# Where the sums of the feed-forward weights are formed: VectorE's additions in four buffers, or adding DMAs in two

## The chip, the cores and the metric

The kernel runs on one core of a Trainium2 chip. The metric is device time in microseconds (us) of the whole program; the median of three executions before the change is 2494.41 us (2494.4 to 2494.79). The engines are named as the profile names them: PE is TensorE (matmuls), PEld its weight loads, DVE VectorE, ACT ScalarE, POOL GpSimd, and SP SyncE, whose queue issues nearly all DMAs here. A line such as L1243 is a line of the kernel.

## The reference

One step of a hybrid decoder layer of width 1024, for 2048 prompt tokens and 8 sample sequences of 8 tokens, which share the weights:

```python
h = rmsnorm(x, norm_mix_w)
proj = h @ w_in          # rq, rk, rv, rg (RetNet), hq, hf, hi, hg (HGRN2), 512 columns each
o_r, s_ret = chunk_gla(rotary(rq), rotary(rk) * 128**-0.5, rv, log(1 - 2**(-5-h)), s_ret0)
f = lb + (1 - lb) * sigmoid(hf)
o_h, s_hg = chunk_gla(silu(hq) * 128**-0.5, 1 - f, hi, log(f), s_hg0)
o = concat(head_rmsnorm(o_r) * silu(rg), head_rmsnorm(o_h) * silu(hg))
x = x + o @ w_out
h = rmsnorm(x, norm_ffn_w)
x = x + square(relu(h @ w_up)) @ w_down      # 1024 -> 4096 -> 1024
y = rmsnorm(x, final_norm_w)
```

`chunk_gla` is a gated linear recurrence in chunks, four heads of each kind with 128 dimensions. Everything is float32, and the four new states are outputs too.

## The kernel before

**Arithmetic.** The kernel forms each float32 product from split operands: every weight and activation is cut into a high part (`hi`, a float32r copy by ACT, L270 for weights) and the rest (`lo`, a subtraction by DVE, L284), and three matmuls (hi by hi, hi by lo, lo by hi) add up in PSUM.

**Order.** Tokens go in three groups of 640, 768 and 704 columns (the last holds the 64 sample rows). First all three groups are mixed: projection (L341), values (L748), the two recurrences and the output projection. Then come three groups of feed-forward (L1211). Group 0 is mixed up to about 394 us, group 1 to about 820 us, group 2 to about 1188 us; the feed-forward takes the rest.

**Feed-forward.** Up and down matrices are cut into 16 sets (8 of each) of four weight tiles A11, A12, A21, A22, each 128x1024 float32 (512 KB). Instead of eight block products, seven are made, by a scheme of Strassen's kind. It needs sums of weight tiles and sums of activation blocks:

```python
S1 = A21 + A22;  S2 = S1 - A11;  S3 = A11 - A21;  S4 = A12 - S2
T1 = B12 - B11;  T3 = B22 - B12; T2 = T3 + B11;   T4 = B21 - T2
PRODUCTS = A11*B11, S2*T2, A12*B21, S3*T3, S1*T1, A22*T4, S4*B22
```

The S sums are made once, in `plan_sums`, while groups 1 and 2 are being mixed (eight sets in each), stored in DRAM tiles `su...` and `sd...` and loaded in the feed-forward as other weights are. The T sums are made by `block_sum` for each group of the feed-forward.

**What sets the order of instructions.** The program is emitted in one pass, and a counter of ticks runs along: one tick for every two matmuls of a projection (three of the values). `plan_sums` puts steps with due ticks in a list, `self.side`; `tick` emits a step when its tick has come, among whatever the mixing emits there. Each engine then runs its own instructions in that order (the steps of the sums are held in program order), so an instruction that waits holds back all that follow it on its engine or queue. Sets start at tick 16 and at 141 + 192*(j//2) + 85*(j%2): after the first, two sets for each 192 ticks, which is one head pair of the mixing. Within a set the steps stand so: loads of A21 and A22 at 0, A11 at 12, A12 at 24 (L1240, SP); S1 at 40, S3 at 50, S2 at 60, S4 at 70 (L1243, DVE); stores at 60, 70, 80, 90 (L1248, SP). The tiles come from a pool with the tag "sum" and four buffers, one set's worth. SP's queue carries, in between, the loads of the weights for the mixing, some of them already split halves kept in DRAM (`w16hi`, `w16lo` and so on, L253).

Other lines that the text speaks of: ACT's evictions L357, its tables L361 and L363, its copies L505, its gate L854; PE's column sums L511 and L512, which need a PSUM bank that L357 empties; POOL's tensor products L705, L713, L894 and L895.

Of the kernel before, what the change touches and what calls it, by code (L numbers as in the profile page):

```python
# [9 lines left out]
F32 = mybir.dt.float32  # L10
F32R = mybir.dt.float32r
U8 = mybir.dt.uint8
AF = mybir.ActivationFunctionType
ALU = mybir.AluOpType

P = 128
# [26 lines left out]
WT = 1024  # L43
# [15 lines left out]

T_SUMS = {"T1": ("B12", ALU.subtract, "B11"), "T3": ("B22", ALU.subtract, "B12"), "T2": ("T3", ALU.add, "B11"),
          "T4": ("B21", ALU.subtract, "T2")}
QUARTER = {(0, 0): "B11", (0, 1): "B12", (1, 0): "B21", (1, 1): "B22"}
PLACE = {name: q for q, name in QUARTER.items()}
A_PLACE = {"A11": 0, "A12": 1, "A21": 2, "A22": 3}
# [133 lines left out]
class Kernel:  # L200
# [36 lines left out]
    def load(self):  # L237
        return self.ld.tile([P, SLAB], F32, tag="ld", name="ld")
# [993 lines left out]
    def plan_sums(self, sets, starts):  # L1232
        nc, w = self.nc, self.I["w"]
        assert not self.side
        self.side = deque()

        def load(x, i, *names):
            for name in names:
                x[name] = self.wp.tile([P, WT], F32, tag="sum", name="raw", bufs=4)
                self.tc.keep_in_program_order(nc.sync.dma_start(x[name], w[i + A_PLACE[name]]))  # L1240

        def make(x, name, a, op, b, into):
            self.tc.keep_in_program_order(nc.vector.tensor_tensor(out=x[into], in0=x[a], in1=x[b], op=op))  # L1243
            x[name] = x[into]

        def keep(x, key, name):
            s = self.sums[key + (name,)] = self.dp.tile([P, WT], F32, name="s" + "".join(map(str, key)) + name)
            self.tc.keep_in_program_order(nc.sync.dma_start(s, x[name]))  # L1248

        for start, (key, i) in zip(starts, sets):  # L1250
            x, t = {}, self.n_ticks + start
            steps = [(0, load, x, i, "A21", "A22"), (12, load, x, i, "A11"), (24, load, x, i, "A12"),
                     (40, make, x, "S1", "A21", ALU.add, "A22", "A22"),
                     (50, make, x, "S3", "A11", ALU.subtract, "A21", "A21"),
                     (60, make, x, "S2", "S1", ALU.subtract, "A11", "A11"),
                     (70, make, x, "S4", "A12", ALU.subtract, "S2", "A12")]
            steps += [(d, keep, x, key, name) for d, name in ((60, "S1"), (70, "S3"), (80, "S2"), (90, "S4"))]
            for d, fn, *a in sorted(steps, key=lambda z: z[0]):
                self.side.append((t + d, lambda fn=fn, a=a: fn(*a)))
        self.side = deque(sorted(self.side, key=lambda z: z[0]))  # L1260

    def out_proj(self, g, when, beside, between=lambda: None):
# [45 lines left out]
        return first, second  # L1308

    def block_sum(self, g, B, name):  # L1310
        a, op, b = T_SUMS[name]
        s = self.get()
        self.nc.vector.tensor_tensor(out=s[:, :g.T], in0=B[a][:, :g.T], in1=B[b][:, :g.T], op=op)  # L1313
        B[name] = s

    def plan_operands(self, g):

# [510 lines left out]
```

## Time and profile before

| | |
|---|---|
| median of three executions | 2494.41 us |
| profiled execution, first to last instruction (span) | 2490.7 us |
| difference of the two | 3.7 us |
| mean granted TensorE clock | 0.999 |
| PE, PEld busy | 2478.4, 2461.9 us (100%, 99%) |
| DVE, ACT, POOL busy | 1868.8, 1246.4, 377.3 us (75%, 50%, 15%) |
| 16 DMA engines, mean busy share of the sync queue's transfers | 62.3% |
| DMA bytes | 525.44 MB |

A group row of the profile reads: line, engine, operation, output tile and input tiles, shapes, count, then busy time and mean ns of one, then the idle time of the engine just before these instructions and what ended it. A row of the waits reads: engine, line, what it waited for; us in total, how often, the longest. A row of a timeline reads: start, duration, engine, line, operation, tiles, how many like it were merged, and in brackets the idle time before it with what ended it; for SP the duration is that of issuing, not of the transfer. A row of DMA issues gives count, KB of each, and the median us from issue to landing.

### The profile page before, as it was taken

Reading aid. Unit: us, or ns where it says so; the run is one execution under the profiler, and the core shown is the slowest. Engines: PE = TensorE matmul, PEld = TensorE weight load, DVE = VectorE, ACT = ScalarE, POOL = GpSimd, SP = SyncE. Lnnn points to the kernel's source line nnn. Section 1 sums busy time; section 2 is a strip of 40 time slices with the busy share of each in tenths; the row PEclk is TensorE's granted clock in tenths of the full one; section 3 lists DMA queues with packets and bytes.
Section 4 is the critical chain, followed back from the end, with each engine's and each line's share of the span. In section 5 each row is a group of like instructions: output and inputs, shape, how many; then the busy total and the mean of one; then the engine's idle time right before and its main releaser. Section 6 shows DMA issues by size and latency. Waiting matters only on the chain.

```text
span 2490.7 us, 41430 instructions
## 1 busy us (share of the span) xinstructions
PE 2478.4 (100%) x16520; PEld 2461.9 (99%) x16520; DVE 1868.8 (75%) x2453; ACT 1246.4 (50%) x1674; POOL 377.3 (15%) x320
## 2 busy tenths in 40 slices
PE   9999999999999999999999999999999999999998
PEld 9999999999999999999999999999999999999998
DVE  7666766667685666686775899776699878778987
ACT  6665663444464444453644545444454436445544
POOL 5223304324421442340000000000000000000000
PEclk9999999999999999999999999999999999999999
DMA  7454575465566665768876866576675545867552
GB/s 265 166 185 170 203 259 178 161 229 186 184 210 236 220 219 200 266 211 270 283 213 221 280 198 213 174 239 222 203 262 177 188 151 190 288 196 247 194 189 89
DMA packets 191655, 525.44 MB, mean 211 GB/s; under 512 B 20963, under 2 KB 62563, under 8 KB 191462
## 3 DMA queue, kind: packets, MB, share of 16 engines
q1 hardware_dynamic: 191318, 522.77, 62.3%
q8 instruction: 130, 2.13, 0.4%
q14 instruction: 63, 0.52, 0.1%
q10 hardware_dynamic: 144, 0.02, 0.0%
HBM read 389.28 MB, written 132.39 MB: 209 GB/s over the span
## 4 chain that ended last, share of the span: by engine, by line
PE 98%; DVE 1%; DMA 0%; ACT 0%; issue 0%; SPq 0%; DVEq 0%
PE pj L341 29%; PE pf L1211 26%; PE pj L1211 25%; PE pjv L748 8%; PE mm L920 2%; PE mm L1108 1%; PE po L1100 1%; PE po L1102 1%; PE mm L977 1%; PE mm L512 1%; PE mm L511 1%; PE po L784 1%; PE mm L1034 1%; PE mm L850 1%; DMA lo<-w33lo 0%; DMA slab<-x 0%
## 5 line engine op out<-in xcount | busy, mean ns | idle before, releaser
L270 ACT CAST hi<-raw 128x1024 fp32r<-128x1024 f32 x392 | 411.8, 1050 | 616.6 <-PE pf L1211 258.4
L341 PE MATMUL pj<-slab,hi 128*128 128x320 f32 (+2 forms) x3072 | 661.4, 328 | 1.8 <-DVE slab L649 1.0
L1211 PE MATMUL pf<-slab,hi 128*128 128x320 f32 (+2 forms) x2768 | 657.6, 321 | 0.0
L1211 PE MATMUL pj<-slab,hi 128*128 128x352 f32 (+2 forms) x2608 | 620.6, 322 | 0.0
L284 DVE TENSOR_TENSOR lo<-raw,hi 128x1024 fp32r<-128x1024 f32 x392 | 485.6, 1239 | 113.6 <-ACT hi L270 108.1
L341 PEld LDWEIGHTS pj<-slab,hi 128*128 128x128 f32 x3072 | 508.3, 188 | 3.9 <-DVE slab L649 1.2
L1211 PEld LDWEIGHTS pf<-slab,hi 128*128 128x128 f32 x2768 | 480.1, 188 | 0.0
L1211 PEld LDWEIGHTS pj<-slab,hi 128*128 128x128 f32 x2608 | 452.9, 188 | 0.1
L1211 PE MATMUL pf<-slab,lo 128*128 128x320 f32 (+2 forms) x1384 | 444.1, 321 | 0.0
L1211 PE MATMUL pj<-slab,lo 128*128 128x352 f32 (+2 forms) x1304 | 419.1, 321 | 0.0
L341 PE MATMUL pj<-slab,lo 128*128 128x320 f32 (+2 forms) x1536 | 379.5, 327 | 0.5 <-DVE lo L284 0.4
L341 PEld LDWEIGHTS pj<-slab,lo 128*128 128x128 f32 x1536 | 263.6, 188 | 1.6 <-DVE lo L284 1.0
L1211 PEld LDWEIGHTS pf<-slab,lo 128*128 128x128 f32 x1384 | 259.6, 188 | 0.0
L1211 PEld LDWEIGHTS pj<-slab,lo 128*128 128x128 f32 x1304 | 244.6, 188 | 0.0
L748 PE MATMUL pjv<-hi,slab 128*128 128x256 f32 x1024 | 193.3, 285 | 0.0
L1302 ACT CAST slab<-slab 128x640 fp32r<-128x640 f32 (+2 forms) x192 | 145.2, 778 | 64.0 <-DVE slab L1313 51.7
L1306 DVE TENSOR_TENSOR slab<-slab 128x640 fp32r<-128x640 f32 (+2 forms) x192 | 167.0, 884 | 8.5 <-PE pj L1211 2.8
L748 PEld LDWEIGHTS pjv<-hi,slab 128*128 128x128 f32 x1024 | 162.2, 192 | 1.4
L748 PE MATMUL pjv<-lo,slab 128*128 128x256 f32 x512 | 144.8, 283 | 0.0
L899 ACT ACTIVATE slab<-slab 128x640 f32<-128x640 f32 (+2 forms) x72 | 56.3, 782 | 147.7 <-POOL slab L895 147.4
L1556 DVE TENSOR_TENSOR slab<-pf,slab 128x640 f32<-128x640 f32 (+2 forms) x88 | 77.5, 886 | 29.4 <-PE pf L1211 28.9
L748 PEld LDWEIGHTS pjv<-lo,slab 128*128 128x128 f32 x512 | 98.1, 192 | 0.0
(222 smaller groups left out, 3009.0 us busy)
## 6 DMA issues: line engine op xcount, KB each, us to landing
raw<-w SPq DMA_DIRECT2D x264, 512.0 KB, 4.3
slab<-u SPq DMA_DIRECT2D x32, 384.0 KB, 4.8
u<-ld SPq DMA_DIRECT2D x30, 384.0 KB, 4.0
slab<-u SPq DMA_DIRECT2D x32, 352.0 KB, 5.0
u<-ld SPq DMA_DIRECT2D x30, 352.0 KB, 3.9
slab<-u SPq DMA_DIRECT2D x32, 320.0 KB, 4.6
u<-ld SPq DMA_DIRECT2D x30, 320.0 KB, 4.3
ld<-x SPq DMA_DIRECT2D x16, 384.0 KB, 3.8
```

Source lines behind the costliest of these rows:

```text
L270: self.nc.scalar.copy(hi, raw)
L284: self.nc.vector.tensor_tensor(out=lo, in0=self.second.pop(j), in1=hi.bitcast(F32), op=ALU.subtract)
L341: self.nc.tensor.matmul(pj[:, i, :T2], w, a[:, c0:c1], start=j == 0 and q == 0, stop=j == n - 1 and q == 2)
L511: self.nc.tensor.matmul(ps, self.ones_r, hi, start=True, stop=False)
L512: self.nc.tensor.matmul(ps, self.ones_r, lo, start=False, stop=True)
L748: nc.tensor.matmul(pj[:, i * 256:(i + 1) * 256], a[:, s:s + C], ww, start=kb == 0 and q == 0, stop=kb == KB - 1 and q == 2)
L899: nc.scalar.activation(x["dd", w][:, a:T], x["dd", w][:, a:T], AF.Exp)
L920: nc.tensor.matmul(ps[:, j], qk[:, cols[c]], second(qk[:, cols[c]]), start=True, stop=True)
L1211: self.nc.tensor.matmul(*a, **k)
L1302: self.nc.scalar.copy(hi[:, :g.T], B[name][:, :g.T])
L1306: self.nc.vector.tensor_tensor(out=lo[:, :g.T], in0=B[name][:, :g.T], in1=hi.bitcast(F32)[:, :g.T], op=ALU.subtract)
L1556: nc.vector.tensor_tensor(out=r, in0=ps, in1=r, op=ALU.add)
```

## The change

The sums S are formed by DMAs that add to what stands in their destination (`accum_op`), issued from GpSimd's queue, and only A21 and A22 have buffers. In this way, with the signs that can be had by additions alone:

- SP loads A21 and A22 (ticks 0 and 1). ACT negates both in place, a Copy activation with scale -1 over 128x1024 (ticks 14 and 16).
- Tick 22: A22's buffer += A21's buffer, SBUF to SBUF, which makes -S1; stored at 34.
- Tick 36: A21's buffer += A11 from DRAM, which makes S3; stored at 48.
- Tick 46: A22's buffer += A11 from DRAM, which makes -S2; it may begin once the store of -S1 has landed; stored at 58.
- Tick 70: A22's buffer += A12 from DRAM, which makes S4; it may begin once the store of -S2 has landed; stored at 82.

S1 and S2 are negated, so T1 and T2 are, too: T1 is B11 - B12, T2 is -T3 - B11 in one scalar_tensor_tensor, T4 is B21 + T2. The seven products have the values they had. The pool with the tag "sum" keeps its four buffers, so that two sets fit in it. The starts of the sets are as they were. The scratch for dynamic DMAs is 512 instead of 256.

```diff
-T_SUMS = {"T1": ("B12", ALU.subtract, "B11"), "T3": ("B22", ALU.subtract, "B12"), "T2": ("T3", ALU.add, "B11"),
-          "T4": ("B21", ALU.subtract, "T2")}
+T_SUMS = {"T1": ("B11", ALU.subtract, "B12"), "T3": ("B22", ALU.subtract, "B12"), "T4": ("B21", ALU.add, "T2")}
...
-        def load(x, i, *names):
-            for name in names:
-                x[name] = self.wp.tile([P, WT], F32, tag="sum", name="raw", bufs=4)
-                self.tc.keep_in_program_order(nc.sync.dma_start(x[name], w[i + A_PLACE[name]]))
-        def make(x, name, a, op, b, into):
-            self.tc.keep_in_program_order(nc.vector.tensor_tensor(out=x[into], in0=x[a], in1=x[b], op=op))
-            x[name] = x[into]
...
+        def load(x, i, name):
+            x[name] = self.wp.tile([P, WT], F32, tag="sum", name="raw", bufs=4)
+            order(nc.sync.dma_start(x[name], w[i + A_PLACE[name]]))
+        def negate(x, name):
+            order(nc.scalar.activation(x[name], x[name], AF.Copy, scale=-1.0))
+        def add(x, name, term):
+            order(nc.gpsimd.dma_start(x[name], x[term] if isinstance(term, str) else w[term], accum_op=ALU.add))
...
-            steps = [(0, load, x, i, "A21", "A22"), (12, load, x, i, "A11"), (24, load, x, i, "A12"),
-                     (40, make, x, "S1", "A21", ALU.add, "A22", "A22"),
-                     (50, make, x, "S3", "A11", ALU.subtract, "A21", "A21"),
-                     (60, make, x, "S2", "S1", ALU.subtract, "A11", "A11"),
-                     (70, make, x, "S4", "A12", ALU.subtract, "S2", "A12")]
-            steps += [(d, keep, x, key, name) for d, name in ((60, "S1"), (70, "S3"), (80, "S2"), (90, "S4"))]
...
+            for d, fn, *a in ((0, load, i, "A21"), (1, load, i, "A22"), (14, negate, "A21"), (16, negate, "A22"),
+                              (22, add, "A22", "A21"), (34, keep, "A22", key + ("S1",)), (36, add, "A21", i + A_PLACE["A11"]),
+                              (46, add, "A22", i + A_PLACE["A11"]), (48, keep, "A21", key + ("S3",)),
+                              (58, keep, "A22", key + ("S2",)), (70, add, "A22", i + A_PLACE["A12"]),
+                              (82, keep, "A22", key + ("S4",))):
...
+        if name == "T2":
+            self.nc.vector.scalar_tensor_tensor(out=s[:, :T], in0=B["T3"][:, :T], scalar=-1.0, in1=B["B11"][:, :T],
+                                                op0=ALU.mult, op1=ALU.subtract)
+            return
...
-    nc = _bacc.Bacc("TRN2", target_bir_lowering=False, num_devices=1, dynamic_dma_scratch_size=256)
+    nc = _bacc.Bacc("TRN2", target_bir_lowering=False, num_devices=1, dynamic_dma_scratch_size=512)
```

More of the change, by code (lines that the diff above doesn't have):

```diff
@@ L1235, in plan_sums @@
         self.side = deque()
-        def load(x, i, *names):
-            for name in names:
-                x[name] = self.wp.tile([P, WT], F32, tag="sum", name="raw", bufs=4)
-                self.tc.keep_in_program_order(nc.sync.dma_start(x[name], w[i + A_PLACE[name]]))
-        def make(x, name, a, op, b, into):
-            self.tc.keep_in_program_order(nc.vector.tensor_tensor(out=x[into], in0=x[a], in1=x[b], op=op))
-            x[name] = x[into]
-        def keep(x, key, name):
-            s = self.sums[key + (name,)] = self.dp.tile([P, WT], F32, name="s" + "".join(map(str, key)) + name)
-            self.tc.keep_in_program_order(nc.sync.dma_start(s, x[name]))
+        order = self.tc.keep_in_program_order
@@ new lines, in load, with keep @@
+        def load(x, i, name):
[5 more added lines that the diff above has]
+            order(nc.gpsimd.dma_start(x[name], x[term] if isinstance(term, str) else w[term], accum_op=ALU.add))
+        def keep(x, name, key):
+            s = self.sums[key] = self.dp.tile([P, WT], F32, name="s" + "".join(str(k) for k in key))
+            order(nc.sync.dma_start(s, x[name]))
@@ L1257, in plan_sums @@
-            steps += [(d, keep, x, key, name) for d, name in ((60, "S1"), (70, "S3"), (80, "S2"), (90, "S4"))]
-            for d, fn, *a in sorted(steps, key=lambda z: z[0]):
-                self.side.append((t + d, lambda fn=fn, a=a: fn(*a)))
+            for d, fn, *a in ((0, load, i, "A21"), (1, load, i, "A22"), (14, negate, "A21"), (16, negate, "A22"),
[3 more added lines that the diff above has]
+                              (82, keep, "A22", key + ("S4",))):
+                self.side.append((t + d, lambda fn=fn, a=a, x=x: fn(x, *a)))
@@ L1310, in block_sum @@
     def block_sum(self, g, B, name):
+        s = self.get()
+        B[name], T = s, g.T
+        if name == "T2":
+            self.nc.vector.scalar_tensor_tensor(out=s[:, :T], in0=B["T3"][:, :T], scalar=-1.0, in1=B["B11"][:, :T],
+                                                op0=ALU.mult, op1=ALU.subtract)
+            return
         a, op, b = T_SUMS[name]
-        s = self.get()
         self.nc.vector.tensor_tensor(out=s[:, :g.T], in0=B[a][:, :g.T], in1=B[b][:, :g.T], op=op)
-        B[name] = s
     def plan_operands(self, g):
```

## The prediction

> **What bounds the kernel now.** I read in this order: busy time and the chain that ended last, then TensorE's (PE's) own waits, the busy time in the two stretches that hold the sums, and the timelines of SP, ACT and POOL where one set hands over to the next.
>
> ```profile
> span 2490.7 us, 41430 instructions
> PE 2478.4 (100%) x16520; PEld 2461.9 (99%) x16520; DVE 1868.8 (75%) x2453; ACT 1246.4 (50%) x1674; POOL 377.3 (15%) x320
> ...
> q1 hardware_dynamic: 191318, 522.77, 62.3%
> ...
> PE 98%; DVE 1%; DMA 0%; ACT 0%; issue 0%; SPq 0%; DVEq 0%
> ```
>
> PE is busy all the time and is 98% of the chain. What it waited for is the whole of this list:
>
> ```profile
> PE mm L408 <- DVE eps L412: 1.1, 1, 1.1
> PE pj L341 <- DVE slab L649: 1.0, 1, 1.0
> PE pf L1755 <- ACT slab L1746: 0.8, 1, 0.8
> PE pj L341 <- DVE slab L1271: 0.8, 1, 0.8
> PE pj L341 <- DVE lo L284: 0.4, 1, 0.4
> ```
>
> That is 4.1 us, none of it behind a weight sum (L1243) or its loads and stores. The sums are made in the mixing of groups 1 and 2; there the engines stood so (columns: busy us of PE, weight loads, DVE, ACT, POOL; clock; DMA share; GB/s):
>
> ```profile
> 394.00:820.00 426.00, 426.00 (x2933) 421.44 (x2932) 290.10 (x421) 198.55 (x290) 142.50 (x109) 1.00 0.56 199
> 820.00:1188.00 368.00, 367.01 (x2644) 361.76 (x2643) 255.61 (x442) 169.36 (x280) 115.95 (x109) 1.00 0.69 234
> ```
>
> PE has under 1 us free in 794 us, so time can only be lost here: there is nothing behind PE to give back. The measured median is 2494.4 us, which leaves 3.7 us outside the profiled span; I add changes to 2494.4.
>
> **The change part by part.**
>
> ```profile
> L1243 DVE TENSOR_TENSOR raw<-raw 128x1024 f32<-128x1024 f32 x64 | 90.2, 1410 | 0.3
> L270 ACT CAST hi<-raw 128x1024 fp32r<-128x1024 f32 x392 | 411.8, 1050 | 616.6 <-PE pf L1211 258.4 <-PE pj L1211 207.0 <-issue 76.3
> L1313 DVE TENSOR_TENSOR slab<-slab 128x768 f32<-128x768 f32 x32 | 29.7, 950 | 0.0
> L1401 DVE SCALAR_TENSOR_TENSOR ld<-ld 128x768 f32<-128x768 f32 x14 | 13.3, 950 | 0.0
> raw<-w SPq DMA_DIRECT2D x264, 512.0 KB, 4.3
> ```
>
> *DVE.* 64 additions go, 64 x 1.41 = 90.2 us of an engine that is 68% busy (290.1 of 426) where they stand and releases no PE wait there. Gain: 0. T2 as a SCALAR_TENSOR_TENSOR costs 950 ns as the TENSOR_TENSOR did; T1's turned sign costs nothing. Cover: DVE's free third.
>
> *ACT.* 32 negations of 128x1024 at 1.05 us (the same tile in L270) = 33.6 us on an engine half idle. Free by themselves. But each now waits in ACT's order for a load, and PE stands behind ACT; that price comes below.
>
> *The larger DMA scratch* adds no instruction: 0. *PE's own order:* in group 2 the sample heads' matmuls move a few places; 0, at most a wait of the size listed (1 us).
>
> *DMA traffic.* A set had four loads and four stores; it has two loads, four stores and four accumulates, of which three fetch from DRAM. 525 MB took 62.3% of 16 engines over 2490.7 us, so 0.524 MB takes 1.55 us of all of them; two to six more such passes per 44 us (an accumulate counted as one pass or two) make 3 to 9 us, which lifts the share of 0.56 to 0.69 by 0.07 to 0.2. It stays under 1 and prolongs other loads, at no cost of its own while these are fetched early.
>
> *The hand-over, where the change can cost.* In two buffers the sums form a chain, each step waiting for the one before: S1 is added in A22 (one accumulate) and kept, only then can A11 be added onto it (S2), kept, then A12 (S4), kept. Three accumulates (A) and two stores (S) are serial: x = 3A + 2S + five hand-overs. Behind it in SP's order stand the next set's two loads, and behind them in ACT's order that set's negations. In the profile:
>
> ```profile
> 502.31 5.60 SPq L1240 DMA_DIRECT2D raw<-w  x2
> 508.00 0.38 SPq L253 DMA_DIRECT2D hi<-w16hi  x1
> ...
> 590.41 5.05 SPq L1240 DMA_DIRECT2D raw<-w  x2
> ```
> ```profile
> 511.75 0.58 ACT L854 ACTIVATE slab<-mm,con 128x384 f32<-128x384 f32 x1 [0.84 <-PE mm L850]
> ```
> ```profile
> 545.56 0.52 ACT L505 CAST slab<-slab 128x384 fp32r<-128x384 f32 x1
> 546.10 1.28 ACT L361 ACT_TABLE_LOAD   x1
> 549.40 0.84 ACT L361 ACTIVATE slab<-slab 128x768 f32<-128x768 f32 x1 [2.02 <-DVE slab L649]
> 550.26 1.28 ACT L363 ACT_TABLE_LOAD   x1
> 552.18 0.58 ACT L357 ACTIVATE slab<-mm,eps 128x384 f32<-128x384 f32 x1 [0.64 <-PE mm L512]
> 555.63 0.58 ACT L357 ACTIVATE slab<-mm,eps 128x384 f32<-128x384 f32 x1 [2.31 <-PE mm L512]
> ```
>
> The loads of one pair of sets to the next are 590.41 - 502.31 = 88.1 us apart: 44 us a set, eight pairs in all (four per group; group 2 a little shorter). In each pair the first set's negations go in beside L854, done by about 513 (511.75 + 0.58 + the negation), and the first accumulate starts there. The second set's first negation stands right behind L505 (545.56 + 0.52 = 546.1). Its 1.05 us fit in ACT's 2.02 us wait before L361; beyond that the delay runs through L361 and the L357 of 552.18 to PE, whose next L511 (about 555.1, as the L357 it releases starts at 555.63) is in need of that bank some 2.3 us after L357 gave it up. So the second set's A21 must have landed by about 549.4. It is issued at 513 + x and takes a load's 4.3 us: nothing is lost up to x = 549.4 - 513 - 4.3 = 32.1. Above that ACT stands, PE behind it, and every us of x beyond 32.1 is a us of the kernel in each of eight pairs. From a second set to the next first set there are 88.1 - (549.4 - 513) = 51.7 us, which binds only when x is some 15 us longer.
>
> Now A and S. A store of a sum, alone and bunched, with the fastest and slowest landing of this line's transfers in one pair:
>
> ```profile
> su7S<-raw SPq DMA_DIRECT2D x4, 512.0 KB, 5.2
> sd00S<-raw SPq DMA_DIRECT2D x4, 512.0 KB, 7.2
> sd01S<-raw SPq DMA_DIRECT2D x4, 512.0 KB, 4.2
> sd20S<-raw SPq DMA_DIRECT2D x4, 512.0 KB, 5.7
> ...
> DMA to landing us min/median/max: 2.6/7.8/9.7
> ```
>
> S: 5.45, the middle of 4.2 to 7.2 and of the two between. Hand-overs: the issue of a DMA takes SP 0.32 to 0.38 us; five of them 1.6. No queue of GpSimd and no accumulate is in the trace (the queue that moves all but 3 MB is q1). The nearest row is the same 512 KB as a plain load, 4.3 us; a plain pass alone took 2.6, which is the lower end of A; two passes at the bunched worst, 19.4, are the upper. An accumulate reads two tiles and writes one where a copy reads and writes one: 1.5 x 4.3 = 6.5, or, if it goes as two passes, 8.6. I take the middle, 7.5, as an estimate.
>
> x = 3 x 7.5 + 2 x 5.45 + 1.6 = 35.0, which is 2.9 us over 32.1; times eight is 23 us: 2494.4 + 23 = 2517. The price turns on A: A = 6.5 gives x = 32.0 and no loss at all, A = 10 gives x = 42.5 and 83 us.
>
> The Trainium skill, Collectives: The Full Stack (Stop ④, why ReduceScatter is half of AllGather), says that an adding transfer is slower because it needs two source reads, and its DMA page, DMA: Bandwidth & Descriptors (Anatomy of one DMA), gives about 2.0 us plus bytes over 436 GB/s for a transfer from GpSimd. From these two, an estimate: 2.0 + 2 x 1.2 = 4.4 us for one accumulate that is alone, and by that A the sum would be 2494; no run here shows an accumulate.
>
> Other work behind the waits: SP's loads of hi/lo weights (w18 to w21) stand among the keeps, and POOL's tensor products (L705, L713, L894) behind the accumulates' waits. POOL is idle for two thirds of these windows (142.5 of 426), and the first of its products after the chain is wanted later than the second set's load, so they bind after it; taken as 0.
>
> **Rivals.**
>
> *Hidden: no change.* If A is 6.5 or less with S as taken, the chain ends in time, and ACT's waits and SP's fall in idle time. For it: the fastest landing is 2.6, and two loads a set bunch less than four. Against: the median in a pair was 7.8. Time 2494.4, within 2 us.
>
> *Accumulates far slower, chain over a set's whole share.* If GpSimd cannot feed its queue while VectorE works beside it, A grows towards 12 or more. Then the chain from loads to loads, 4.3 + 2.1 (two negations) + x, is the pace itself: at A = 12, x = 48.5 and the set 54.9 us, 10.9 over its 44; sixteen sets, 174 us: 2669. Decides from x = 44 - 6.4 = 37.6 on, A about 8.4. For it: DVE is 68% busy there. Against: no DMA of the trace, bunched with others, took over 9.7. The Trainium skill's SBUF — State Buffer (the "DVE blocks DMA" trap) states such a rule for DMAs issued from GpSimd: their descriptors cannot be written while VectorE runs an operation in a two-port mode. No trace here shows it yet.
>
> *Faster.* With 90 us off DVE, a PE wait on DVE in these two groups would go. The listed waits on DVE are 1.1 + 1.0 + 0.8 + 0.4 = 3.3 us; even all of them gone gives 2491.1, and by the windows only 1 us of it lies in the sums' stretches. It needs over 5 us to count as faster; only a change in how fast PE streams could do that, and I see none.
>
> **How the numbers follow.** A change below 0.2% (5 us) cannot be told from none; in eight pairs that is 0.6 us each, so x up to 32.7, A up to 6.7. Chances by A: up to 6.7, 0.38; 6.7 to about 10, the hand-over as the loss, 0.40; above 10, the chain as the pace, 0.18; faster 0.04. The forecast is the second: 2517, its own range 2500 to 2577 (A = 10). The range for 8 in 10 takes in the hidden case and ends just above the second: 2492 to 2580. Same 0.38, slower 0.58, faster 0.04.
>
> **What would show it.** L1243 gone from DVE, its busy time down by 90 us; 32 more Copy activations near 1.05 us. A queue of GpSimd with 64 issues, landing at about 7.5 us. In the waits, ACT waiting for a load at the second set of each pair, some 3 us each time, and PE's L511/L512 waiting on ACT's L357 eight times; SP standing before the keeps. Right on the mechanism and wrong on size if A is another; wrong altogether if PE waits for something else, such as a weight half (hi/lo) that SP fetched late behind a keep, or a POOL product behind an accumulate, or if PE slows with no wait at all.

## The result, and the profile after

The changed kernel takes 2559.97 us in the median of four runs (2555.32 to 2575.8), against 2494.49 us before (four runs): 1.0276 times the time, 95% interval 1.0261 to 1.0291, which is 65 us slower. The prediction said 2517 us, 2492 to 2580, slower with 0.58: side and range hold, the size is short by almost a factor of three. The profiled execution is the slowest of the four, 2575.8 us, 16 us above the median; what follows splits up this execution.

From its page, the span, TensorE's (PE's) line, the queue of GpSimd's DMAs and their landing times (median, us):

```profile
span 2574.0 us, 41479 instructions
PE 2513.3 (98%) x16520; PEld 2490.4 (97%) x16520; DVE 1810.2 (70%) x2389; ACT 1277.9 (50%) x1706; POOL 400.3 (16%) x384
...
q0 software_dynamic: 9216, 33.56, 7.6%
...
raw<-w POOLq DMA_DIRECT2D x48, 512.0 KB, 7.8
```

The span is 83.3 us longer than before. Of this 48.4 us are PE standing still (span less busy time, 60.7 us against 12.3), and 34.9 us are the same 16520 matmuls taking longer. In the two stretches of mixing that hold the sums (columns as before the change):

```profile
394.00:820.00 426.00, 402.90 (x2683) 396.30 (x2683) 248.34 (x375) 199.81 (x291) 138.43 (x130) 0.96 0.68 198
820.00:1188.00 368.00, 347.01 (x2417) 338.36 (x2416) 198.93 (x353) 166.82 (x263) 134.39 (x141) 0.96 0.79 226
```

PE is now idle 44 us in these 794 us, where it was idle for one, and the granted clock is 0.96 where it was 1.00. PE's own waits (what it waited for: us in total, times, longest) were five rows of 4.1 us; the largest now are:

```profile
PE mm L976 <- DVE slab L905: 16.8, 5, 4.0
PE po L783 <- POOL slab L776: 8.7, 3, 3.5
PE mm L510 <- ACT slab L356: 5.6, 3, 2.5
PE po L783 <- DMA ld<-hg_s: 5.3, 1, 5.3
PE pjv L741 <- DMA lo<-w5lo: 3.8, 1, 3.8
PE mm L510 <- ACT slab L504: 3.2, 3, 2.6
```

(The lines of this kernel are one lower than before up to the sums: L976 is the former L977, L356 the former L357.) Three things stand in this list, and a fourth behind it.

**VectorE held up by GpSimd.** The largest row ends in L905, a short product that VectorE forms of two tiles in SBUF. The minimum, median and maximum of L904, the product ahead of it, in ns, in the changed kernel and in the kernel before (there L905):

```profile
L904 DVE TENSOR_TENSOR slab<-slab x72: 477/547/8858, 48.7 to 1182.3; 128x320 f32<-128x320 f32 x40, 128x384 f32<-128x384 f32 x24, 128x352 f32<-128x352 f32 x8
```
```profile
L905 DVE TENSOR_TENSOR slab<-slab x72: 477/650/1258, 48.6 to 1107.8; 128x320 f32<-128x320 f32 x40, 128x384 f32<-128x384 f32 x24, 128x352 f32<-128x352 f32 x8
```

An operation of half a microsecond took 8.86. The timelines of VectorE and of GpSimd at that place:

```profile
504.09 8.86 DVE L904 TENSOR_TENSOR slab<-slab 128x384 f32<-128x384 f32 x1 [2.40 <-ACT slab L898]
512.88 0.55 DVE L905 TENSOR_TENSOR slab<-slab 128x384 f32<-128x384 f32 x1
```
```profile
502.35 0.84 POOL L894 TENSOR_TENSOR slab<-slab 128x384 f32<-128x384 f32 x1
503.83 0.89 POOL L1246 DMA_DIRECT2D raw<-w  x1 [0.64 <-DMA su2S<-raw]
504.43 1.51 POOL L948 TENSOR_TENSOR slab<-slab 128x384 f32<-128x384 f32 x1
...
511.36 1.17 POOL L894 TENSOR_TENSOR slab<-slab 128x384 f32<-128x384 f32 x1
```

GpSimd issues an adding DMA at 503.83 and then runs eight operations without a break until 512.53. (L893 and L894 are differences of two tiles, L948 and L926 products; "products" means the whole run here, as in the expectations.) VectorE's operation starts 0.3 us after that issue has begun and comes to its end 0.4 us after the run. This happens eight times, four in each group, with 6.2 to 10.1 us each (L904 three times, L951 three times, L713 twice; all of them combine two tiles in SBUF). In the kernel before, GpSimd has runs of 11 to 13 us at the same places, and 8 to 11 operations of VectorE fall into each, none longer than 2.2 us.

**The chain of a set, and what waits behind it.** From GpSimd's, SP's and ScalarE's timelines, the set su3:

```profile
531.59 0.89 POOL L1246 DMA_DIRECT2D raw<-raw  x1 [2.26 <-ACT raw L1243]
536.63 0.89 POOL L1246 DMA_DIRECT2D raw<-w  x1 [4.15 <-DMA raw<-raw]
...
545.48 0.89 POOL L1246 DMA_DIRECT2D raw<-w  x1 [6.46 <-issue]
...
558.22 0.89 POOL L1246 DMA_DIRECT2D raw<-w  x1 [9.98 <-DMA su3S<-raw]
```
```profile
564.89 0.32 SPq L1250 DMA_DIRECT2D su3S<-raw  x1
565.27 1.19 SPq L1240 DMA_DIRECT2D raw<-w  x2
```
```profile
571.00 1.06 ACT L1243 ACTIVATE raw<-raw 128x1024 f32<-128x1024 f32 x1 [5.60 <-DMA raw<-w]
```

From the first accumulate to the next set's loads 565.27 - 531.59 = 33.7 us; when the first of those loads has landed ScalarE's negation starts, at 571.0, ScalarE has stood still for 5.6 us, and PE then waits 2.5 us for L356. That is the step on which the prediction rested. But GpSimd stands in the same chain (10 us before 558.22), with L776 behind it in group 2; and SP stands in it, with weight halves (w5) and the sample states (hg_s) behind it.

**The clock.** PE's granted clock (last column but two) around three pauses of PE, of 4.04, 2.54 and 1.44 us:

```profile
509.44:513.50 4.06, 0.02 (x1) 0.03 (x1) 4.06 (x3) 0.06 (x1) 3.09 (x3) 0.80 0.00 0
513.50:516.00 2.50, 2.50 (x14) 2.38 (x15) 2.50 (x6) 2.08 (x4) 0.00 (x0) 0.50 0.00 0
516.00:518.00 2.00, 2.00 (x12) 1.66 (x12) 0.24 (x1) 0.43 (x2) 0.00 (x0) 0.50 0.00 0
518.00:520.00 2.00, 2.00 (x16) 2.00 (x16) 0.00 (x0) 0.00 (x0) 0.00 (x0) 0.81 0.17 29
```
```profile
574.57:577.11 2.54, 0.00 (x0) 0.00 (x0) 0.00 (x0) 2.50 (x4) 1.71 (x2) 0.93 0.00 0
577.11:579.11 2.00, 2.00 (x6) 2.00 (x7) 0.56 (x1) 1.42 (x3) 0.79 (x1) 0.50 0.39 80
579.11:581.11 2.00, 2.00 (x12) 2.00 (x12) 0.56 (x1) 0.29 (x2) 0.00 (x0) 0.73 0.95 186
479.85:482.00 2.15, 2.15 (x13) 2.15 (x14) 0.87 (x2) 1.61 (x3) 0.80 (x1) 1.00 0.46 93
```

After the pause of 4 us PE runs at half clock for nearly 5 us, which costs another 2.6 us; after 2.5 us it loses some 1.5 us; after 1.4 us nothing. Read in the same way in windows of half a microsecond, the profile has twelve such stretches in these two groups, each behind a pause of 2.5 us or more, and together they cost some 31 of the 34.9 us of longer matmuls (an estimate from PE's busy time and its clock in each window). Over the whole run that makes (48.4 + 34.9) / 48.4, about 1.7 times the length of the pauses.

### The profile page after: what moved, and what is told of

It is laid out like the page before. It is cut to its first block, busy times and chain, and to the rows that moved or that the text cites. A ratio compares the mean times of both kernels' runs of the same rounds, so it can differ in the third digit from the quotient of the medians.

```text
span 2574.0 us, 41479 instructions
## 1 busy us (share of the span) xinstructions
PE 2513.3 (98%) x16520; PEld 2490.4 (97%) x16520; DVE 1810.2 (70%) x2389; ACT 1277.9 (50%) x1706; POOL 400.3 (16%) x384
## 4 chain that ended last, share of the span: by engine, by line
PE 52%; DVE 0%; DMA 0%; ACT 0%; DVEq 0%; issue 0%
PE pf L1210 26%; PE pj L1210 24%; PE pj L340 2%; DMA ld<-hg_s 0%; DVE slab L1667 0%; PE po L783 0%; DVE slab L1766 0%; PE po L1101 0%; PE mm L1107 0%; PE po L1099 0%; PE pf L1759 0%; DVE slab L1624 0%; PE pj L511 0%; PE pj L510 0%; PE mm L834 0%; ACT slab L1700 0%
## 5 line engine op out<-in xcount | busy, mean ns | idle before, releaser
L340 PE MATMUL pj<-slab,hi 128*128 128x320 f32 (+2 forms) x3072 | 668.4, 331 | 0.8 <-DVE slab L1271 0.8
L747 PE MATMUL pjv<-hi,slab 128*128 128x256 f32 x1024 | 203.1, 295 | 0.0
L747 PEld LDWEIGHTS pjv<-hi,slab 128*128 128x128 f32 x1024 | 170.5, 201 | 1.8
```

Source lines behind the costliest of these rows:

```text
L340: self.nc.tensor.matmul(pj[:, i, :T2], w, a[:, c0:c1], start=j == 0 and q == 0, stop=j == n - 1 and q == 2)
L747: nc.tensor.matmul(pj[:, i * 256:(i + 1) * 256], a[:, s:s + C], ww, start=kb == 0 and q == 0, stop=kb == KB - 1 and q == 2)
```

## The experiments

All times are medians; before, on the same chips, 2492.7 to 2494.7 us. Two theories of the first set: L, the hold on VectorE comes from a DMA that GpSimd issues ahead of a run; W, it comes from GpSimd's waiting, which piles up its products.

**1. A store issued by GpSimd ahead of the run, in the kernel before.**

```diff
...
+            if start in [16] + [226 + 192 * k for k in range(3)]:
+                steps[7] = (70.5, keep, x, key, "S1", nc.gpsimd)
...
-            self.tc.keep_in_program_order(nc.sync.dma_start(s, x[name]))
+            self.tc.keep_in_program_order((queue or nc.sync).dma_start(s, x[name]))
```

> The kernel before, with one store in eight of the sixteen sets (the store of S1, which waits for nothing by then) issued by GpSimd ahead of its run of tensor products instead of by SP. Theory L (after GpSimd has issued a DMA, VectorE cannot run until GpSimd's unbroken run of tensor products ends): eight VectorE instructions of 6 to 10 us, eight waits of TensorE of 2 to 4 us and a halved clock behind each; 2525 to 2560 us. Theory W (the loss comes from GpSimd's waits for adding DMAs, which pile up its products): no instruction of VectorE over 2.9 us, TensorE's waits 4 us in all, 2493 to 2497 us.

Measured: 2530.02 us, 1.0146 times (1.0131 to 1.0161). PE's largest wait, and timelines of GpSimd and VectorE:

```profile
PE mm L977 <- DVE slab L906: 22.8, 6, 4.2
```
```profile
491.42 0.60 POOL L1248 DMA_DIRECT2D su2S<-raw  x1
492.05 1.21 POOL L949 TENSOR_TENSOR slab<-slab 128x384 f32<-128x384 f32 x1
```
```profile
492.39 7.88 DVE L905 TENSOR_TENSOR slab<-slab 128x384 f32<-128x384 f32 x1 [2.40 <-ACT slab L899]
```

The DMA waited for nothing, adds nothing and lasted 0.6 us on GpSimd; VectorE was held for 7.1 to 7.9 us at six of the eight places (at the other two GpSimd paused between the store and its run). Eight stores moved to another queue, six of them ahead of a run, cost 37 us. Theory L holds.

**2. GpSimd waits, without a DMA.**

```diff
...
+                steps[2] = (64, load, x, i, "A12")
+                steps[6] = (86, make, x, "S4", "A12", ALU.subtract, "S2", "A12")
+                steps[10] = (98, keep, x, key, "S4")
+                steps += [(70.5, touch, x, "A12")]
...
+        def touch(x, name):
+            self.tc.keep_in_program_order(nc.gpsimd.tensor_copy(self.spare, x[name][:, :1]))
```

> The kernel before, with GpSimd made to wait for the load of A12 at the same eight places (it copies one column of the tile, the load is issued six ticks ahead, S4 is made and stored later); GpSimd issues no DMA. Theory L: no VectorE instruction over 2.9 us, TensorE's waits under 10 us, 2494 to 2503 us. Theory W: the products pile up behind the wait and hold VectorE up as in the changed kernel, 2515 to 2560 us.

Measured: 2516.04 us. The products of VectorE (L905 before), and what VectorE waited for:

```profile
L906 DVE TENSOR_TENSOR slab<-slab x72: 476/1026/1377, 49.5 to 1129.7; 128x320 f32<-128x320 f32 x40, 128x384 f32<-128x384 f32 x24, 128x352 f32<-128x352 f32 x8
```
```profile
DVE raw L1244 <- POOL spare L1252: 23.0, 4, 7.9
```

No hold. But the copy did not stand where it was meant to. At the two places with a long run behind (waits of 5.1 and 4.9 us) GpSimd paused twice more, 0.9 to 1.9 us each, before that run began; at the other six only two to five operations followed without a break (2.6 to 4.8 us). And in group 2 the making of S4 waited for the copy on VectorE: PE paused three times, 15 us and its clock. So this run does not decide between the theories. It tells that waits of 5 to 8 us made no hold over runs of up to 4.8 us, and that an in-order wait of 5 to 8 us in group 2 reaches PE. That a hold needs no wait of GpSimd is shown by experiment 1.

**3. The last adding DMA behind the run.**

```diff
...
-  (70, add, "A22", i + A_PLACE["A12"]),
-  (82, keep, "A22", key + ("S4",))):
+  ((162 if start == 16 else 131) if start in late else 70, add, "A22", i + A_PLACE["A12"]),
+  ((174 if start == 16 else 143) if start in late else 82, keep, "A22", key + ("S4",))):
```

> The changed kernel, with the last adding DMA of those eight sets (A12 onto A22) issued after GpSimd's run of tensor products instead of ahead of it; its store follows later. Theory L: the eight long VectorE instructions and TensorE's waits behind them (L905, L504; 20 us and a clock loss of some 2.5 us each) are gone, 2515 to 2535 us. Theory W: the adding DMAs still wait ahead of other GpSimd work, 2545 to 2562 us.

Measured: 2579.38 us, slower than the changed kernel. The longest L904 is now 1.5 us, the holds are gone, but PE waits for:

```profile
PE mm L510 <- ACT slab L356: 15.5, 3, 5.3
PE po L783 <- POOL slab L776: 9.5, 3, 4.9
PE mm L510 <- ACT slab L347: 9.4, 4, 6.0
```

The later end of the chain seems to have pushed the next set's steps into the work behind them. The time lies above both forecasts: the two causes trade against each other.

**4. The loads ahead.**

```diff
-            for d, fn, *a in ((0, load, i, "A21"), (1, load, i, "A22"), (14, negate, "A21"), (16, negate, "A22"),
+            for d, fn, *a in ((-16, load, i, "A21"), (-15, load, i, "A22"), (14, negate, "A21"), (16, negate, "A22"),
```

> The changed kernel, with a set's two loads sixteen ticks earlier, so that they stand on SP's queue ahead of the last store of the set before. By the prediction's own step (a second set's load comes late behind the chain, ScalarE's negation waits for it, TensorE waits for L356) this takes away TensorE's waits on L356, 5.6 us in the profile, and the clock behind them: 2545 to 2553 us. If that step is worth nothing, 2555 to 2562 us.

Measured: 2570.29 us. The time lies above both forecasts. The wait on L356 is gone, as the prediction's step would have it, and no time is won:

```profile
PE po L783 <- DMA ld<-hg_s: 20.4, 5, 5.9
```

The sample states' loads are late on SP's queue instead.

**5. The store ahead of a pause.** Experiment 1 with another tick:

```diff
-                steps[7] = (70.5, keep, x, key, "S1", nc.gpsimd)
+                steps[7] = (46, keep, x, key, "S1", nc.gpsimd)
```

> As the first experiment (the kernel before, eight stores of S1 issued by GpSimd), but each store is issued 24 ticks earlier, ahead of a product (L713) after which GpSimd stands idle for its next operands. Theory L (the hold on VectorE lasts until GpSimd's unbroken run of products ends): the run is one product, no VectorE instruction over 4 us, TensorE's waits under 6 us, 2493 to 2500 us. If a DMA issued by GpSimd holds VectorE by itself, or until the transfer has landed: VectorE instructions of 4 us and more at these places, 2510 to 2530 us.

Measured: 2493.54 us, 1.0002 times (0.9992 to 1.0011). GpSimd's timeline, and the products of VectorE:

```profile
478.45 0.60 POOL L1248 DMA_DIRECT2D su2S<-raw  x1 [1.39 <-PE mm L512]
484.19 1.85 POOL L713 TENSOR_TENSOR slab<-slab,ld 128x768 f32<-128x768 f32 x1 [5.13 <-ACT slab L656]
```
```profile
L905 DVE TENSOR_TENSOR slab<-slab x72: 477/631/1257, 48.7 to 1107.8; 128x320 f32<-128x320 f32 x40, 128x384 f32<-128x384 f32 x24, 128x352 f32<-128x352 f32 x8
```

Behind the DMA GpSimd now stands idle for 5 us (3.5 to 5.6 us at the eight places), and the long run that follows later holds nobody. A transfer in flight is not what holds either: in group 2 L1243, which combines two tiles in SBUF, starts on VectorE 0.3 us behind three of these stores and takes 1.2 us, no more than its mean of 1.4 in the kernel before. The same eight stores cost 37 us in one place and nothing in another. The larger DMA scratch, which experiments 1 and 5 have too, costs nothing either.

**6. The sample queries on VectorE** (L776).

```diff
-            self.nc.gpsimd.tensor_copy(z, q[:, 32 * i:32 * i + 32].rearrange("p (s r) -> p s r", r=SLEN))
+            self.nc.vector.tensor_copy(z, q[:, 32 * i:32 * i + 32].rearrange("p (s r) -> p s r", r=SLEN))
```

> The changed kernel, with the copies of the sample queries (L776) made by VectorE instead of GpSimd, so that they no longer stand behind an adding DMA that waits for a store. Theory: TensorE's waits on L776 (8.7 us in three, with a slower clock behind each, some 16 us in all) are gone, 2540 to 2552 us. If they only make room for another wait at the same place (the states' loads late on SP's queue, the sums of VectorE), 2553 to 2565 us.

Measured: 2565.06 us (2557.3 to 2569.85), no gain. The wait on L776 is gone and this one stands in its place:

```profile
PE po L783 <- DMA ld<-hg_s: 8.8, 3, 4.2
```

**7. Copying instead of adding.**

```diff
-            order(nc.gpsimd.dma_start(x[name], x[term] if isinstance(term, str) else w[term], accum_op=ALU.add))
+            order(nc.gpsimd.dma_start(x[name], x[term] if isinstance(term, str) else w[term]))
```

> The changed kernel, with GpSimd's 64 DMAs copying instead of adding, everything else in its place (the sums, and with them the outputs of the feed-forward, are not computed). GpSimd's DMAs land in 3.5 to 5 us instead of a median of 7. If the length of the chain sets the waits on SP's queue, on L356 and on L776: these waits go down from 27 us to under 10 and the kernel takes 2515 to 2540 us; the eight holds on VectorE stay, with their 20 us of TensorE's waits. If the length doesn't matter, 2553 to 2562 us.

This kernel leaves out the sums, so it measures time only. Measured: 2520.0 us (2517.19 to 2524.32). GpSimd's DMAs and PE's largest wait:

```profile
raw<-w POOLq DMA_DIRECT2D x48, 512.0 KB, 5.2
```
```profile
PE mm L976 <- DVE slab L905: 16.7, 6, 3.1
```

The DMAs from DRAM land 2.6 us earlier (7.8 to 5.2), and all waits but those behind the holds, six here, go under 1.2 us each. So some 40 us of the 65 hang on adding instead of copying, which shows in the profile as longer DMAs, and the other 25 are the holds: 16.7 us of waits, and 8 us of clock by the half-microsecond windows.

**8. Other ticks for all steps.** Both sets of a pair are loaded ahead, the adding DMAs alternate, stores stand some 20 ticks behind the sums:

```diff
...
+        plan = ((-14, -13, 0, 2, 6, 26, 22, 36, 42, 50, 58, 78),
+                (-30, -29, 10, 12, 24, 44, 40, 54, 60, 74, 86, 106),
+                (-109, -108, -69, -67, -53, -33, -37, -23, -17, -3, 15, 47))
...
```

> The changed kernel with other ticks: both sets of a pair are loaded ahead of the pair, their eight adding DMAs alternate between GpSimd's long runs of products, and every store stands some 20 ticks behind its sum. If the losses are the three that the traces show (holds on VectorE by a DMA ahead of a run, GpSimd's products behind a waiting DMA, SP's loads behind a waiting store) and the clock behind each: 2494 to 2512 us. If the adding DMAs cost by themselves (traffic, buffers), 2525 us and more.

Measured: 2591.74 us, the slowest of all; that lies in the second branch, though not for the reason given there, as experiment 9 shows. Two holds are left, one at the start of each group. The largest waits belong to the sample rows of group 2, whose steps stand behind adding DMAs and negations:

```profile
PE po L783 <- POOL slab L776: 26.3, 3, 9.4
PE mm L806 <- ACT slab L803: 18.5, 4, 6.1
```

**9. Experiments 3 and 7 together:** both diffs, nothing else; the sums are left out here, too.

> The third and the seventh experiment together: the changed kernel with copying instead of adding DMAs (the sums, and with them the feed-forward's outputs, are not computed) and the last one of the eight sets behind GpSimd's run of products. If the two causes, the hold on VectorE and the length of the chain of adding DMAs, are all of the loss: no VectorE instruction over 4 us ahead of a run, TensorE's waits under 8 us, 2494 to 2503 us. If there is a third cause (the negations on ScalarE, two buffers, GpSimd's DMAs as such): 2510 us and more.

Measured: 2495.36 us (2493.19 to 2497.52), 1.0008 times (0.9999 to 1.0018). PE's largest wait is 1.9 us. With neither hold nor long accumulates nothing is left: the negations, the two buffers, GpSimd's 64 DMAs as such and the turned signs cost nothing that can be measured. The two shares, 40 and 25 us, are those of this order, first the length, then the hold; taking the hold away alone (experiment 3) won nothing.

**10. Half of the sets adding.** The eight sets of the holds are summed by VectorE in four buffers:

```diff
...
+            if start in late:
+                steps = ((0, load, i, "A21"), (0.1, load, i, "A22"), (12, load, i, "A11"), (24, load, i, "A12"),
+                         (40, make, "A22", "A21", -1.0, ALU.subtract, "A22"), (50, make, "A21", "A21", -1.0, ALU.add, "A11"),
+                         (60, make, "A11", "A22", 1.0, ALU.add, "A11"), (60.1, keep, "A22", key + ("S1",)),
+                         (70, make, "A12", "A12", 1.0, ALU.add, "A11"), (70.1, keep, "A21", key + ("S3",)),
+                         (80, keep, "A11", key + ("S2",)), (90, keep, "A12", key + ("S4",)))
...
```

> The changed kernel with the eight sets whose last adding DMA stands ahead of GpSimd's run summed by VectorE in four buffers, as before the change (with the signs of the change); the other eight sets keep the adding DMAs, now one chain for each 88 us instead of two. If the loss comes from the hold and from chains that follow one another too closely: no hold, TensorE's waits under 8 us, 2493 to 2505 us. If each chain costs by itself, half of what the holds do not explain, some 20 us: 2512 us and more.

Measured: 2521.92 us, by the second branch; but the cost is not spread over the chains. Group 1 has no pause of 1 us. In group 2 PE pauses four times (11.5 us by the rows, where the next expectation has 12.3, and 14 us of clock), three of them for

```profile
PE po L783 <- POOL slab L776: 10.0, 3, 3.9
```

**11. The same with the sample queries on VectorE:** the diff of experiment 6 on top of 10.

> The tenth experiment with the copies of the sample queries (L776) made by VectorE. All that TensorE still waits for there beyond the kernel before is L776 behind an adding DMA on GpSimd (10.0 us in the waits, 12.3 us of pauses, and 14 us of clock behind them). If that is the whole rest: no such wait, 2493 to 2500 us. If another wait takes its place, as in the sixth experiment: 2505 us and more.

Measured: 2514.52 us. Once more the next one in the row steps forward, this time behind a store on SP's queue:

```profile
PE po L783 <- DMA ld<-hg_s: 8.6, 4, 3.0
```

**12. The store behind the states.** On top of 11, for its eight chains:

```diff
...
-  (58, keep, "A22", key + ("S2",)), (70, add, "A22", i + A_PLACE["A12"]), (82, keep, "A22", key + ("S4",))
+  (76, keep, "A22", key + ("S2",)), (86, add, "A22", i + A_PLACE["A12"]), (96, keep, "A22", key + ("S4",))
```

> The eleventh experiment with the store of S2, the last adding DMA and the store of S4 of its eight chains 18, 16 and 14 ticks later, so that the loads of the sample states (L768) stand ahead of the store of S2 on SP's queue. TensorE's waits on these loads (8.6 us, 9.9 us of pauses, 8.6 us of clock behind them) should go, and with them what is left: 2493 to 2500 us. If the later end of the chain makes another wait (the next set's loads on SP for buffers, L356): 2503 us and more.

Measured: 2498.15 us (2495.77 to 2500.9), 1.0019 times (1.001 to 1.0029). Its accumulates land no faster, and PE's wait on the states is down to 1 us:

```profile
raw<-w POOLq DMA_DIRECT2D x24, 512.0 KB, 8.1
```
```profile
PE po L783 <- DMA ld<-hg_s: 1.0, 1, 1.0
```

So eight sets can be summed by adding DMAs at almost no cost (5 us here) if nothing urgent stands behind any of their waits. None of the versions was faster than the kernel before.

## Why the prediction was right on the side and short on the size

*Nothing to gain.* Right. VectorE's busy time fell by 59 us (1868.8 to 1810.2; the holds count as busy, and in experiment 9, without holds, it fell by 82), and nothing got earlier. T2, T1, the negations (L1243, 1.06 us each) and the larger scratch cost nothing by themselves: experiment 9.

*The length of an accumulate.* Right: 7.5 us taken, 7.8 measured for the 48 that fetch from DRAM, 5.2 for the 16 inside SBUF. The Trainium skill's DMA: Bandwidth & Descriptors and Collectives: The Full Stack together had led to an estimate of 4.4 us for one alone. One alone was not tried: the shortest in the changed kernel landed after 4.4 us, but inside SBUF, and the shortest from DRAM after 5.5.

*The chain.* It was taken as 35.0 us, from the first accumulate to the next set's loads, and is 33.6 to 33.8 in the three pairs of group 1 and 37.8 to 39.0 in those of group 2. That it came so near is in part luck, since its terms were others. The sum had three accumulates and two stores in series. In the profile all four accumulates of a set are in series: each begins only after the one before it has landed, and the third does so within 0.4 us of that landing in 15 of the 16 sets (why, no run shows). In the set su3 they take 4.6, 8.5, 9.1 and 6.7 us from issue to landing, and only one store stands between, of 2.9 us where 5.45 was taken. The accumulate that was left out and the stores that were priced too high nearly cancel.

*The hand-over to ScalarE.* Right in kind, near in price, not in number: 2.9 us were expected at each of eight pairs. By the starts of the sets there are only six such hand-overs, three in each group, since the first and the last set of a group stand apart. PE waits for L356 at the three of group 1, 1.4 to 2.5 us, 5.6 us in all, and at none of group 2, though the chain is longer there. Experiment 4 took the wait away, and another stood there.

*Other work behind the waits, "taken as 0".* This is the step that failed. GpSimd's idle share of two thirds was taken as cover for its products, and the weight halves on SP's queue were not followed to the matmuls that need them, though they were named as a sign of being wrong; but an in-order queue does not spend its idle share where the wait is. In the changed kernel L776, the states and w5 stood behind a waiting DMA or store, 17.8 us of PE's waits in the rows shown above; in experiment 8 L803 did, too. Together with the hand-over, through the length of the accumulate, this is some 40 us (experiment 7).

*What no step had.* The hold on VectorE by GpSimd's run behind a DMA: 16.8 + 3.2 us of PE's waits, some 25 us with the clock in experiment 7, where six holds are left. Nothing in the trace before could show it, since no DMA there is issued by GpSimd. And the clock: each pause was priced at its length, while here it costs about 1.7 times that. The prediction's 23 us would have been some 39 us by that alone (an estimate).

*The rivals.* "Accumulates far slower" was built on VectorE keeping GpSimd's queue from being fed; accumulates of 12 us did not come (the longest landing of GpSimd's DMAs is 10.0 us), and it was the other way round: GpSimd kept VectorE from running. "Hidden" fell: A would have had to be under 6.7 us. "Faster" fell as argued.

## What to carry to other kernels

When a wait is put into an engine's or a queue's order, follow the next few entries behind it one by one, each with its own slack to the matmul that needs it; an idle share of the engine says nothing about that place, and when one of them is repaired the next one shows (L776, then the states, in experiments 6, 10, 11, 12). Price a pause of TensorE with the clock behind it. As far as these runs go, a DMA issued by GpSimd should stand where GpSimd is about to pause, not directly ahead of a run of its operations while VectorE is needed.

## What the runs showed of the hardware

After GpSimd has issued a DMA of 512 KB (adding, copying or storing made no difference), the next operation of VectorE on two tiles in SBUF was held until GpSimd's unbroken run of operations had ended: 6 to 10 us behind eight or eleven operations in the changed kernel, 7.1 to 7.9 us in experiments 1 and 7, nothing in experiment 5, where GpSimd paused for 3.5 to 5.6 us behind each DMA. Without a DMA ahead of it the same run lets VectorE through operation by operation (at most 2.2 us). The Trainium skill's SBUF — State Buffer (SBUF: two separate sides) states that GpSimd and a VectorE operation with two inputs in SBUF share a pair of ports as an exclusive lock, held for the whole of an instruction. The kernel before agrees with that, its operations alternating. Behind a DMA the lock, if it is that, is held over eight or eleven instructions. Why the DMA makes the difference was not tried.

In the changed kernel the granted clock went to 0.50 behind all pauses of 2.5 us and more and stayed at 1.00 behind those of 1.4, 1.6 and 2.1 us. The length alone does not decide: in experiment 11 a pause of 2.05 us was followed by 0.50, in experiment 10 one of 1.6 us, while in experiment 7 two of three pauses of 2.5 us were not. The Trainium skill's TensorE: Matmul & The Clock Gate (What's actually happening) gives about 3.4 us idle for the step to half clock. Here less was enough: 2.54 us at 574.57, where the mean clock of 0.93 in the pause shows that it had fallen before PE went on.

An adding DMA of 512 KB issued by GpSimd took 7.8 us (median) beside this kernel's traffic, the same DMA without the addition 5.2 us (experiment 7), and inside SBUF 5.2 and 2.9 us. The adding DMAs of a set landed one after the other, never two at a time.
